# Attention in a hybrid decoder layer: the order of scores and turning in a two-deep pipeline, and the slot of the turned probabilities

## The chip, the cores and the metric

The kernel runs on one core of one Trainium2 chip. The metric is the time of one execution on the device in microseconds (us); less is better. All inputs lie in the device's memory at the start and the output lies there at the end.

## What is computed

The reference is one layer of a decoder on x of 1 x 1024 x 1024 (batch, sequence, model width), all in 32-bit floats:

```python
h = rmsnorm(x, norm1_w)
proj = h @ w_in                       # columns of mixer A, then of mixer B
# mixer A: causal short conv on q, k, v; gated delta rule over 4 heads of 128; gated RMSNorm
o_a = (rmsnorm(gated_delta_rule(qa, ka, va, g, beta), gdn_norm_w) * silu(z)).reshape(B, S, 512)
# mixer B: 8 heads of 64; causal windows (128, 1), (512, 4), (2048, 16) as (window, dilation)
o_b = dilated_attention(qb, kb, vb)   # the three branches merged by their softmax denominators
x = x + concatenate([o_a, o_b], -1) @ w_out
h = rmsnorm(x, norm2_w)
u = causal_dwconv(h @ w_up, ffn_conv_w)          # width 3, 2 x 2816 columns
x = x + (silu(u[..., :2816]) * u[..., 2816:]) @ w_down
return rmsnorm(x, final_norm_w)
```

The change concerns mixer B, the dilated attention, alone. A query at position t sees the keys t, t-d, ..., t-window of each branch; numerators and denominators of the three branches are added with a common maximum.

## The kernel before

**Layout and products.** Activations are kept transposed (channels on the 128 partitions, time along the row). Each large matrix product is made of three: both factors are split into a high part of a shorter format (fp32r) and a low rest, and hi x hi, hi x lo and lo x hi are added up in PSUM. The helper `mm3` (L196) issues such a triple, `mm` (L187) one product, `tp` (L192) one transpose by the identity matrix. In the profile all products therefore stand at L189 and all transposes at L193; most vector and scalar operations of the streams stand at L139 or L141, those of two wrappers. Which step a row belongs to is read from its tiles: `qT`, `kT` are scores, `ident` with `sm` is turning, `pt` with `vn` values, `pb` with `vc` the merge of classes, `xhi`/`xlo` with `whi`/`wlo` the dense input projection, `ohi` the output projection.

**What sets the order on TensorE (PE).** The steps of the layer are written as generators and given to a recorder, the class `Weave` (L46), with a level each. While the program is written down, the recorder keeps a model time of PE and of the other engines, of when each tile is ready and of when a buffer comes free (`product`, `account`, `slot`). A generator yields how long it will be, in the model, until its next piece can run (`need`, L95: the latest of the named tiles, less PE's model time, plus a slack); `run` (L102) takes, of the generators that are ready, the one of lowest level. So a piece that would have to wait lets pieces of other generators go ahead of it. Attention has level 5 (L1497), the output projection 8, the dense input projection 9: dense products fill the places in which attention is not ready. PE executes in exactly the recorded order (an order token on each product and transpose). The order on the other engines is chosen by a tile scheduler; the attention's softmax operations are issued through `uv` (VectorE, DVE) and `ua` (ScalarE, ACT) with high priority. The model decides the order alone; on the chip every wait is a real one.

**The attention.** There are 4 pairs of heads (`pi`), 2 halves of the sequence (`hh`), and in each half 4 blocks of 128 queries, taken two at a time (u = 0 and 2): 16 pairs of query blocks in all. One pair goes through these steps:

- `scores` (L904): for each of the two blocks and each of the two heads one product into a PSUM bank, for the near keys (the block itself and the one ahead of it), and small products for the far keys, taken in four classes by position modulo 4. The first block's two banks have the tag "asc", the second's "atr". Rows of scores are 128 and 256 columns wide in the first pair of a half-0 group, then 288/320, and 352/384 and 416/448 in half 1.
- `softmax` (L929), issued from within `scores` for each block: on DVE a reduction that adds the mask and finds the largest score, from PSUM to the tile `sm` in SBUF (a custom operation with an accumulator read behind it), one for each head; on ACT the exponentials; on DVE the reciprocal and two scalings.
- `turn` (L945): transposes `sm` on PE, head by head, into PSUM banks of the same two tags, "asc" for the first block and "atr" for the second; each of these four sets waits in the recorder with `need(pp, sm, slack=TSLACK[b])`, TSLACK (L39) being -1.0 and -0.6 us. DVE copies the near part to the tile `pt`, ACT the far part to `pb`.
- `values` (L966): 6 (first pair of a sequence) or 8 products of `pt` with the value tile `vn`, into the bank `po` of the group.
- after the second pair of a half, `merge_classes` (L975; 8 products in half 0, 16 in half 1) adds the far keys by way of `pb` and `vc`, and `give` (L989) copies the result out.

Scores, values and merge are products of plain 32-bit floats, and the trace counts two instructions for each: 20 products of scores are a row of x40, 8 of values x16, 16 of the merge x32. Transposes and dense products are counted once. A few records are missing (x10 where 12 belong).

Each PSUM tag has two banks: "hf", "asc", "ch", "atr".

**The pipeline.** `advance` (L1004) holds one pair back. Called with a new pair, it takes the pair ahead of it from the list `pipe` and does, before the change: turning of the pair ahead, scores (with softmax) of the new pair, values of the pair ahead, and at the end of a half its merge. The last call has no new pair.

**Buffers in SBUF.** `SLOTS` (L26) gives a number of slots to each tag. A tag with a star alternates between two tags, so "dv*" (L27) means two slots of "dv" and two of "dw" in turn. Before the change `sm` (one for each block) and `pt` (one for each pair) both take "dv*". The tag "uy" has five slots and holds, in the attention, q and k of a head pair (two slots for each); the four-head state tile `ct` of mixer A's chain (L798) has one of them before the attention. The lists HTAGS (L28), R1TAGS and R2TAGS (L30, L31) name the slots that the input's normalised copies and the weights of the MLP take over when the earlier users are gone; a tag named there is the slot that a tile gets, and a load into it waits for the slot's last reader.

Of the kernel before, what the change touches and what calls it, by code (L numbers as in the profile page):

```python
# [15 lines left out]
P = 128  # L16
# [6 lines left out]
APART = 0.5  # L23
KSLACK = 1.0
EPS = 1e-6
SLOTS = {"kT": 2, "kU": 2, "dv": 2, "dw": 2, "kt": 4, "uy": 5, "qa": 4, "ev": 2, "go": 2, "Xa": 7, "Xb": 9}  # L26
TURNS = {"kT*": ("kT", "kU"), "dv*": ("dv", "dw"), "X": ("Xa",) * 7 + ("Xb",) * 9}  # L27
HTAGS = ("kU", "kU", "dw", "dw", "kt", "kt", "kt", "kt", "uy", "uy", "uy", "uy", "uy", "qa", "qa", "qa", "qa",  # L28
         "ev", "ev", "go", "go") + ("Xa",) * 7
R1TAGS = ("kU", "kt", "qa", "uy", "kt", "qa", "uy", "ev", "kU", "dw", "uy")  # L30
R2TAGS = ("kt", "kt", "uy", "uy", "qa", "qa", "ev", "go", "go", "dw", "Xa")  # L31
PTAGS = ("Xb",) * 9 + ("Xa",) * 2
TOKEN = "pe"
SLACK = 3.0
# [110 lines left out]
def hybrid_layer(tc, I, out):  # L145
# [17 lines left out]
    def tile_(pool, shape, dt, name, tag, bufs):  # L163
        return wv.slot(pool.tile(list(shape), dt, name=name, tag=tag, bufs=bufs), tag, bufs)
# [3 lines left out]
    def A(name, tag, dt=F32, shape=(P, 1024)):  # L168
        if tag in TURNS:
            i = turns[tag] = turns.get(tag, -1) + 1  # L170
            tag = TURNS[tag][i % len(TURNS[tag])]
        return tile_(lp, shape, dt, name, tag, SLOTS[tag])

# [54 lines left out]
    def rsqrt(dst, src, n):  # L228
        po_.tensor_tensor(dst, src, mhalf[:, :n], op=OP.pow)
# [14 lines left out]
    def bank(tag, name="ps"):  # L244
        return tile_(pp_, (P, 512), F32, name, tag, 2)
# [10 lines left out]
    def v8(t):  # L256
        return t.rearrange("p (c t) -> p c t", c=NCH)
# [206 lines left out]
    def small(name, bufs=2):  # L464
        return tile_(sp, (P, NCH), F32, name, name, bufs)
# [316 lines left out]
    def chain_load(h, s):  # L782
        t = A("qat", "go" if s == 1 and h < 2 else "qa", shape=(P, 2, 512))
        sy.dma_start(t[:, 0, :], qpark[h][:, half(s)])
        sy.dma_start(t[:, 1, :], atpark[h][:, half(s)])
        return t

    ct = []

    def chain(h):  # L790

        for i in range(H):
            yield from wv.until(("m", i))
            yield from wv.until(("v", i))
        d = G[h]
        kT, ktok, vtok, yt, ge, rq, gq, ke = [d[n] for n in ("kT", "ktok", "vtok", "yt", "ge", "rq", "gq", "ke")]
        if not ct:
            ct.append(A("ct", "uy", shape=(P, 8, P)))  # L798
        sts = ct[0][:, 2 * h:2 * h + 2, :]
        qa = chain_load(h, 0)  # L800
        ps = bank(("asc", "ch")[h // 2])
        ms = small("ms", 4)
        tg = str(h)
        st = None
        for c in range(NCH):
            cs = slice(c * P, (c + 1) * P)
            if c == 2 and h < 2:
                qb = chain_load(h, 1)
            if c == 3 and h >= 2:
                yield from wv.until(("c", h - 2, 3))  # L810
                qb = chain_load(h, 1)
            if c == 4:
                qa = qb
            qT, at = [qa[:, i, (c % 4) * P:(c % 4 + 1) * P] for i in range(2)]
            if c == 0:
                r = vtok[:, cs]
                yield wv.need(ps, vtok, yt)
            else:
                yield wv.need(ps, st, slack=HOP)
                mm(ps[:, 0:P], kT[:, cs], st, 0.215)  # L820
                r = tile_(sp, [P, P], F32, "r", "r" + tg, 1)
                uv.scalar_tensor_tensor(r, ps[:, 0:P], ngam[:, c, h:h + 1], vtok[:, cs], op0=OP.mult, op1=OP.add)
                yield wv.need(r, slack=HOP)
            mm(ps[:, P:2 * P], yt[:, c, :], r, 0.215)
            w = tile_(sp, [P, P], F32, "w", "w" + tg, 1)
            if c < NCH - 1:
                wke = tile_(sp, [P, P], F32, "wke", "r" + tg, 1)
                uv.tensor_scalar(wke, ps[:, P:2 * P], ke[:, c:c + 1], None, op0=OP.mult)
            ua.activation(w, ps[:, P:2 * P], AF.Copy)
            if c < NCH - 1:  # L830
                yield wv.need(wke, slack=HOP)
                mm(ps[:, 2 * P:3 * P], ktok[:, cs], wke, 0.215)
                sn = sts[:, c % 2, :]
                if c == 0:
                    uv.tensor_copy(sn, ps[:, 2 * P:3 * P])
                else:
                    uv.scalar_tensor_tensor(sn, st, ge[:, c:c + 1], ps[:, 2 * P:3 * P], op0=OP.mult, op1=OP.add)
            yield wv.need(w, qa, slack=HOP)
            po = yield from next_bank("atr")
            if c:  # L840
                mm(po[:, P:2 * P], qT, st, 0.215)
            mm(po[:, :P], at, w, 0.215)

            ua.activation(vtok[:, cs], po[:, :P], AF.Copy, scale=rq[:, c:c + 1])
            if c:
                uv.scalar_tensor_tensor(vtok[:, cs], po[:, P:2 * P], gq[:, c:c + 1], vtok[:, cs], op0=OP.mult,
                                        op1=OP.add)
            if c < NCH - 1:
                st = sn
            osq = tile_(sp, [P, P], F32, "osq", "osq", 1)  # L850
            ua.activation(osq, vtok[:, cs], AF.Square, accum_out=ms[:, c:c + 1])
            wv.done.add(("c", h, c))

        ve.tensor_scalar(ms, ms, 1.0 / 128, EPS, op0=OP.mult, op1=OP.add)
        rsqrt(ms, ms, NCH)
        po_.tensor_tensor(v8(vtok), v8(vtok), ms[:, :, None].to_broadcast([P, NCH, P]), op=OP.mult)
        wv.add(1, finish(h, vtok))
# [34 lines left out]
    def attention():  # L892
# [50 lines left out]
                uv.tensor_scalar(sm[:, e, :wd], sm[:, e, :wd], den[:, e:e + 1], None, op0=OP.mult)  # L943

        def turn(pair):  # L945
            pts = A("pt", "dv*", shape=(P, 4, 256))
            for b, (it, tag) in enumerate(zip(pair, ("asc", "atr"))):
                sm, near, far = it["sm"], it["near"], it["far"]
                nf = -(-far // P)
                it["pt"] = []  # L950
                for e in range(2):
                    pt = pts[:, 2 * b + e, :]
                    it["pt"].append(pt)
                    pp = bank(tag)
                    yield wv.need(pp, sm, slack=TSLACK[b])
                    for i in range(near // P):
                        tp(pp[:, i * P:(i + 1) * P], sm[:, e, far + i * P:far + (i + 1) * P])
                    for i in range(nf):
                        tp(pp[:, near + i * P:near + (i + 1) * P], sm[:, e, i * P:(i + 1) * P])
                    uv.tensor_copy(pt[:, :near], pp[:, :near])  # L960
                    for i in range(nf):
                        rows = min(far - i * P, P)
                        ua.activation(it["pb"][e][:rows, it["u"], i, :], pp[:rows, near + i * P:near + (i + 1) * P],
                                      AF.Copy)

        def values(pair):  # L966
            yield wv.need(pair[0]["po"], *pair[0]["pt"], slack=-PSLACK)
            for it in pair:
                u = it["u"]
                for i in range(it["near"] // P):  # L970
                    for e, er in enumerate(HALVES):
                        mm(it["po"][er, u * P:(u + 1) * P], v8(it["vn"])[:, it["k0"] // P + i, er],
                           it["pt"][e][:, i * P:(i + 1) * P], 0.11, u == 0 and i == 0, False, skip_group_check=True)
# [29 lines left out]

        def advance(pair):  # L1004
            done = pipe.pop() if pipe else None
            if done is not None:
                yield from turn(done)
            if pair is not None:
                yield from scores(pair)
                pipe.append(pair)  # L1010
            if done is not None:
                yield from values(done)
                if done[1]["u"] == 3:
                    yield from merge_classes(done[0]["g"])
                    give(done[0]["g"])
# [109 lines left out]
    def hblock(name, i):  # L1125
        b = B[name][i] = block(name, HTAGS[hcount[0]])
        hcount[0] += 1
# [229 lines left out]
    def prep(stage, j):  # L1357
        if stage == 0:
# [3 lines left out]
            ops[stage, j] = list(zip(split_pair(g), split_pair(r)))  # L1362
            q = R2[j] = A("r2", R2TAGS[j], shape=(P, 2, 512))
            sy.dma_start(q[:, 0, :], upark[j][:, half(1)])
# [23 lines left out]
        else:  # L1388

            a = raw_tile("wa", ("wst", "whi")[j % 2], wd_rows(j, 1)[:, 1:2], 1)  # L1390
            ops[stage, j] = [(split_one(a[:, 0, :]), split_one(R1[j][:, 1, :], R2TAGS[j]))]

# [169 lines left out]
```

## Time and profile before

| | before |
|---|---|
| median of 3 timed runs | 1223.81 us (1223.63 to 1225.67) |
| profiled execution | 1230.37 us |
| its span | 1228.5 us |
| granted TensorE clock, mean | 0.993 |
| bytes moved by DMA | 154.80 MB, 126 GB/s mean |

The span goes from the first to the last event in the profile; the profiled execution's own time is a little longer. PE is the matrix engine, DVE the vector engine, ACT the scalar engine, POOL GpSimd; SP issues most of the DMAs. In a row of a timeline stand the start in us, the length in us, the engine, the line, the operation, out<-in by the names of the tiles, and in square brackets the idle time of the engine just before it with what ended it. x6 means that six like operations lie behind one another. PE's operations overlap (the next begins before the one ahead has ended), so in a dense stretch the distance from start to start is what a row costs. In a row of groups (line, engine, operation, tiles) come the busy time, the mean of one in ns and the idle time ahead. A row of the windows view has the stretch's start and end, its length, then busy time and (number of operations) of PE, of PE's weight loads, of DVE, ACT and POOL, the granted TensorE clock as a share of full speed, the DMA share and GB/s.

### The profile page before, as it was taken

What the parts mean: (1) busy time and instruction counts of PE and PEld (TensorE: products, weight loads), DVE (VectorE), ACT (ScalarE), POOL (GpSimd) and SP (SyncE); (2) the same over time, 40 slices, a digit from 0 to 9 for tenths busy, and PEclk for the clock granted to TensorE, in tenths of its full rate; (3) what the DMA queues carried; (4) which work ended last, traced back from release to release, by engine and by line L of the source; (5) the groups of instructions that cost most, each with busy time, mean ns of one, the idle gap of its engine ahead of it and who ended that gap; (6) DMA issues with size and microseconds to landing.
All of it is one profiled execution on the core that took longest, in us unless ns stands there. A gap on an engine that the chain in (4) does not pass through costs nothing.

```text
span 1228.5 us, 17935 instructions
## 1 busy us (share of the span) xinstructions
PE 1204.7 (98%) x6848; PEld 993.7 (81%) x6848; DVE 948.3 (77%) x1522; ACT 571.0 (46%) x1115; POOL 51.5 (4%) x58
## 2 busy tenths in 40 slices
PE   9999999999999999999999999999999999999996
PEld 7878887888877777788788888888888878787885
DVE  7675964566476778567888988889888889898875
ACT  7393344356344345555545445444444553344541
POOL 0211010003100000000000000000000000000000
PEclk9999999999999999999999999999999999999998
DMA  7325252345723303344123132231221496455523
GB/s 232 104 76 166 86 142 82 121 132 154 231 84 104 121 27 118 140 138 154 52 86 103 52 103 84 71 103 54 101 93 62 134 370 238 166 164 175 193 86 138
DMA packets 85799, 154.80 MB, mean 126 GB/s; under 512 B 21168, under 2 KB 36304, under 8 KB 85712
## 3 DMA queue, kind: packets, MB, share of 16 engines
q1 hardware_dynamic: 85712, 153.64, 38.8%
q8 instruction: 54, 0.88, 0.3%
q14 instruction: 33, 0.27, 0.1%
HBM read 117.68 MB, written 35.93 MB: 125 GB/s over the span
## 4 chain that ended last, share of the span: by engine, by line
PE 81%; DVE 8%; DMA 5%; issue 2%; ACT 2%; SPq 0%; POOLq 0%; POOL 0%; DVEq 0%; ACTq 0%
PE ps L189 42%; PE pa L189 19%; PE pc L189 9%; PE dw L189 8%; DMA wd<-in_wd 3%; PE ps L193 3%; DVE pr L139 2%; DMA r<-upark 2%; DVE wd L139 1%; DVE x1h L139 1%; DVE kT L139 1%; PE warm L189 1%; ACT dec L139 1%; DMA wst<-in_wu 0%; DVE sm L141 0%
## 5 line engine op out<-in xcount | busy, mean ns | idle before, releaser
L189 PE MATMUL dw<-pr 128*128 128x512 f32 (+1 forms) x984 | 213.4, 378 | 3.5 <-DVE x1h L139 2.3
L189 PEld LDWEIGHTS dw<-pr 128*128 128x128 f32 x984 | 176.1, 188 | 39.7 <-DVE x1h L139 4.4
L189 PE MATMUL ps<-xhi,whi 128*128 128x512 f32 x384 | 160.2, 417 | 0.0
L189 PE MATMUL ps<-xhi,wlo 128*128 128x512 f32 x384 | 150.4, 392 | 0.0
L189 PE MATMUL ps<-xlo,whi 128*128 128x512 f32 x384 | 150.2, 391 | 0.0
L189 PE MATMUL pa<-T,pair 128*128 128x512 f32 x528 | 128.7, 393 | 1.3 <-ACT u L139 1.3
L189 PEld LDWEIGHTS pa<-T,pair 128*128 128x128 f32 x528 | 100.2, 190 | 22.5 <-ACT u L139 1.6
L189 PEld LDWEIGHTS ps<-xhi,wlo 128*128 128x128 f32 x384 | 72.2, 188 | 15.7
L189 PEld LDWEIGHTS ps<-xhi,whi 128*128 128x128 f32 x384 | 72.5, 189 | 14.9 <-issue 2.6
L189 PEld LDWEIGHTS ps<-xlo,whi 128*128 128x128 f32 x384 | 72.7, 189 | 11.2
L139 ACT ACTIVATE u<-pa 128x512 f32<-128x512 f32 x44 | 26.3, 598 | 110.4 <-PE pa L189 110.4
L139 DVE SCALAR_TENSOR_TENSOR y<-xu,fcw,y 128x1023 f32<-128x1023 f32 (+1 forms) x44 | 56.4, 1281 | 25.7 <-ACT y L139 25.6
L139 ACT ACTIVATE whi<-wst 128x1024 fp32r<-128x1024 f32 (+2 forms) x42 | 43.0, 1023 | 68.8 <-PE ps L189 62.4
L189 PE MATMUL pc<-T,S 128*128 128x512 f32 x264 | 63.4, 389 | 0.0
L189 PE MATMUL pa<-B,A 128*128 128x512 f32 x264 | 63.4, 389 | 0.0
L189 PE MATMUL pc<-B,pair 128*128 128x512 f32 x264 | 63.4, 389 | 0.0
L189 PE MATMUL pa<-T,S 128*128 128x512 f32 x264 | 63.4, 389 | 0.0
L141 ACT ACTIVATE sm<-sm,mx 128x128 f32<-128x128 f32 (+7 forms) x64 | 35.5, 555 | 58.8 <-DVE mx L141 58.8
L139 DVE TENSOR_TENSOR wst<-wst 128x512 f32<-128x512 f32 x88 | 60.5, 688 | 0.8
L189 PE MATMUL ps<-B,pair 128*128 128x512 f32 x252 | 60.5, 389 | 0.0
L139 DVE TENSOR_TENSOR wlo<-wst,whi 128x1024 fp32r<-128x1024 f32 (+2 forms) x42 | 49.4, 1177 | 13.2 <-ACT whi L139 13.0
L139 ACT ACTIVATE pr<-wd 128x1024 fp32r<-128x1024 f32 x33 | 34.9, 1059 | 51.9 <-PE dw L189 23.1
(238 smaller groups left out, 2363.7 us busy)
## 6 DMA issues: line engine op xcount, KB each, us to landing
wst<-in_wu SPq DMA_DIRECT2D x44, 512.0 KB, 3.7
wd<-in_wd SPq DMA_DIRECT2D x44, 512.0 KB, 4.2
upark<-y SPq DMA_DIRECT2D x22, 512.0 KB, 3.7
wst<-in_wi SPq DMA_DIRECT2D x21, 512.0 KB, 3.7
r<-upark SPq DMA_DIRECT2D x11, 512.0 KB, 8.1
r<-upark SPq DMA_DIRECT2D x22, 256.0 KB, 7.1
wa<-in_wd SPq DMA_DIRECT2D x22, 256.0 KB, 2.7
wst<-in_wv SPq DMA_DIRECT2D x8, 512.0 KB, 3.7
```

Of the source, the lines that this page charges most:

```text
L139: return getattr(eng, op)(*a, **kw)
L141: return getattr(eng, op)(*a, **kw)
L189: tc.stamp_issue_order_token(nc.tensor.matmul(dst, lhs, rhs, start=start, stop=stop, **kw).ins, TOKEN)
L193: tc.stamp_issue_order_token(nc.tensor.transpose(dst, src, ident).ins, TOKEN)
```

## The change

In `advance` the scores of the new pair now come first, and the turning of the pair ahead follows them; values and merge stay behind turning. The tile `pt` leaves the rotating tag "dv*" and has a tag "ux" of one slot. That slot is taken from "uy", which goes from five to four; the three other users of the fifth slot (`ct`, one of HTAGS, one of R2TAGS) are named "ux".

```diff
-SLOTS = {"kT": 2, "kU": 2, "dv": 2, "dw": 2, "kt": 4, "uy": 5, "qa": 4, "ev": 2, "go": 2, "Xa": 7, "Xb": 9}
+SLOTS = {"kT": 2, "kU": 2, "dv": 2, "dw": 2, "kt": 4, "uy": 4, "ux": 1, "qa": 4, "ev": 2, "go": 2, "Xa": 7, "Xb": 9}
-HTAGS = ("kU", "kU", "dw", "dw", "kt", "kt", "kt", "kt", "uy", "uy", "uy", "uy", "uy", "qa", "qa", "qa", "qa",
+HTAGS = ("kU", "kU", "dw", "dw", "kt", "kt", "kt", "kt", "uy", "uy", "uy", "uy", "ux", "qa", "qa", "qa", "qa",
-R2TAGS = ("kt", "kt", "uy", "uy", "qa", "qa", "ev", "go", "go", "dw", "Xa")
+R2TAGS = ("kt", "kt", "uy", "ux", "qa", "qa", "ev", "go", "go", "dw", "Xa")
@@ chain
-            ct.append(A("ct", "uy", shape=(P, 8, P)))
+            ct.append(A("ct", "ux", shape=(P, 8, P)))
@@ turn
-            pts = A("pt", "dv*", shape=(P, 4, 256))
+            pts = A("pt", "ux", shape=(P, 4, 256))
@@ advance
             done = pipe.pop() if pipe else None
-            if done is not None:
-                yield from turn(done)
             if pair is not None:
                 yield from scores(pair)
                 pipe.append(pair)
             if done is not None:
+                yield from turn(done)
                 yield from values(done)
```

The orders as recorded on PE, from the first scores to the first product of the output projection, with S scores, T transposes, V values, M class merge, F dense products, and the number of each:

```
before: S4 F12 T2 F6 T4 F6 S20 V6 T12 F9 S20 V8 M8 F12 T6 F3 T6 F6 S20 V8 F15 T8 F3 T8 F6 S4 V8 M16
        ... F9 T16 V8 M16
after:  S4 F12 S20 F3 T2 F3 T4 F9 V6 S20 T12 F12 V8 M8 S20 T6 F3 T6 F12 V8 S4 T16 F9 V8 M16
        ... S20 F6 T6 F3 T6 F12 V8 M8 S20 T6 F3 T6 F12 V8 T16 F6 V8 M16 F99
```

Ahead of the attention the order is the same on every engine. F has 342 products there in both, in 44 stretches before and 28 after.

## The prediction

> **What bounds the kernel now.** I began with the page: TensorE is the busy engine, and the question is which of its microseconds are stalls that this change could take away.
>
> ```profile
> PE 1204.7 (98%) x6848; PEld 993.7 (81%) x6848; DVE 948.3 (77%) x1522; ACT 571.0 (46%) x1115; POOL 51.5 (4%) x58
> ```
>
> The PE timeline puts the attention from 329.81 us (first scores) to 484.69 us (first product of the output projection). In it, dense input-projection products fill the places between the attention's small ones. I write S, T, V, M and F for scores, turning (transposes), values, class merge and dense filler. The view of PE's waits between 325 and 510 us starts with this row:
>
> ```profile
> PE ps L193 <- DVE sm L141: 2.0, 2, 1.7
> ```
>
> So turning waits for softmax hardly ever: twice, 2.0 us. That is all the reordering can take away directly, plus what those waits drag behind them. The PE timeline at that place:
>
> ```profile
> 341.07 1.33 PE L193 MATMUL ps<-ident,sm 128*128 128x128 f32 x6 [1.74 <-DVE sm L141]
> 342.67 1.51 PE L193 MATMUL ps<-ident,sm 128*128 128x128 f32 x6 [0.26 <-DVE sm L141]
> 343.83 0.78 PE L189 MATMUL ps<-xhi,whi 128*128 128x512 f32 x1
> 344.41 0.53 PE L189 MATMUL ps<-xlo,whi 128*128 128x512 f32 x1
> 344.78 0.39 PE L189 MATMUL ps<-xhi,wlo 128*128 128x512 f32 x1
> ```
>
> The same work undisturbed, ten microseconds later (start to start: six transposes 0.57, the first F after them 0.31, the next 0.23):
>
> ```profile
> 352.58 0.82 PE L193 MATMUL ps<-ident,sm 128*128 128x128 f32 x6
> 353.15 0.47 PE L189 MATMUL ps<-xhi,whi 128*128 128x512 f32 x1
> 353.46 0.39 PE L189 MATMUL ps<-xlo,whi 128*128 128x512 f32 x1
> 353.69 0.39 PE L189 MATMUL ps<-xhi,wlo 128*128 128x512 f32 x1
> ```
>
> From 339.33 (341.07 less the gap of 1.74) to 344.78 is 5.45 us; undisturbed it is 2 x 0.57 + 0.31 + 0.23 = 1.68. The place loses 3.77 us, more than the gap, because the granted clock (ninth number: 0.50) fell to half:
>
> ```profile
> 342.00:344.00 2.00, 1.74 (x9) 1.37 (x9) 1.57 (x5) 0.53 (x2) 0.00 (x0) 0.50 0.00 0
> ```
>
> Two more places lose time: the last long S, and the last pair, which has no filler left.
>
> ```profile
> 472.74 2.60 PE L189 MATMUL ps<-kT,qT 64*128 64x256 f32 x40
> 475.27 1.09 PE L189 MATMUL ps<-pt,vn 128*64 128x128 f32 x16
> ...
> 478.48 1.91 PE L193 MATMUL ps<-ident,sm 128*128 128x128 f32 x16
> ...
> 484.69 0.50 PE L189 MATMUL ps<-ohi,whi 128*128 128x512 f32 x1
> ```
>
> Lengths elsewhere, from a short S (0.86), V of a pair (0.92) and M of a second half (1.59):
>
> ```profile
> 403.19 0.93 PE L189 MATMUL ps<-kT,qT 64*128 64x128 f32 x8
> 404.05 1.09 PE L189 MATMUL ps<-pt,vn 128*64 128x128 f32 x16
> 404.97 1.66 PE L189 MATMUL ps<-pb,vc 128*64 128x128 f32 x32
> 406.56 0.50 PE L189 MATMUL ps<-xhi,whi 128*128 128x512 f32 x1
> ```
>
> and from the long S with what follows it (1.41, 1.60 and 1.82 us for the three sizes):
>
> ```profile
> 374.07 1.47 PE L189 MATMUL ps<-kT,qT 64*128 64x256 f32 x40
> 375.48 0.77 PE L189 MATMUL ps<-pt,vn 128*64 128x128 f32 x10
> ...
> 383.31 1.68 PE L189 MATMUL ps<-kT,qT 64*128 64x256 f32 x40
> 384.91 1.09 PE L189 MATMUL ps<-pt,vn 128*64 128x128 f32 x16
> ...
> 392.89 1.89 PE L189 MATMUL ps<-kT,qT 64*128 64x256 f32 x40
> 394.71 1.09 PE L189 MATMUL ps<-pt,vn 128*64 128x128 f32 x16
> ```
>
> The S at 472.74 takes 2.53 instead of 1.82 (loss 0.71). The tail takes 6.21 instead of 16 x 0.095 + 0.92 + 1.59 = 4.03 (loss 2.18). **All stalls the change could take away: 3.77 + 0.71 + 2.18 = 6.66 us.** Everywhere else PE runs from one group into the next.
>
> **The change part by part.**
>
> *Removed.* T no longer follows the previous V, so it no longer waits for the softmax of the S before it; in the built order an S and several F lie between. I give the change all 6.66 us. The tail goes too: in the built order the attention ends 33 triples of F (99 products) before the output projection, instead of none.
>
> *Added: T behind S waits for its PSUM banks.* S takes both banks of "asc" and both of "atr"; T, now next, takes the same four. Each of its four sets of transposes must wait until the first softmax step (the custom DVE reduction) has read its bank. Before, the reductions ran under V and F. In the built order, of the 15 turns that follow an S, two follow with an F run between and thirteen directly. PE runs in order, so whatever F stands behind T waits with it. When the reductions start, in DVE's timeline:
>
> ```profile
> 375.52 0.46 DVE L141 CUSTOM_DVE_ANT_0 sm<-ps,mk 128x288 f32<-128x288 f32 x1 [2.21 <-PE ps L189]
> 375.90 0.45 DVE L141 CUSTOM_DVE_ANT_0 sm<-ps,mk 128x288 f32<-128x288 f32 x1
> ...
> 384.86 0.53 DVE L141 CUSTOM_DVE_ANT_0 sm<-ps,mk 128x352 f32<-128x352 f32 x1 [2.26 <-PE ps L189]
> 385.31 0.52 DVE L141 CUSTOM_DVE_ANT_0 sm<-ps,mk 128x352 f32<-128x352 f32 x1
> ...
> 394.55 0.59 DVE L141 CUSTOM_DVE_ANT_0 sm<-ps,mk 128x416 f32<-128x416 f32 x1 [2.52 <-PE ps L189]
> 395.06 0.59 DVE L141 CUSTOM_DVE_ANT_0 sm<-ps,mk 128x416 f32<-128x416 f32 x1
> ...
> 403.71 0.29 DVE L141 CUSTOM_DVE_ANT_0 sm<-ps,mk 128x128 f32<-128x128 f32 x1 [1.36 <-PE ps L189]
> ```
>
> Measured from the end of S (the start of PE's next row), the first reduction starts at +0.04, -0.05, -0.16 and -0.34 us, and they follow each other every 0.38, 0.45, 0.51 and about 0.22 us (the second of a pair's blocks is some 0.03 slower). A set can start about 0.2 us after its reduction's successor could (0.08 for the accumulator read, the rest my estimate of the hand-over). So, with a transpose at 0.095:
> - S of 288/320 then T of 1, 1, 2, 2: sets start at 0.62, 1.00, 1.41, 1.82 and end at 2.02, against 0.57: 1.45 lost, three times = 4.35. (The first such S has F around both halves: 0.16.)
> - S of 352/384 then twelve transposes: 0.60, 1.04, 1.52, 2.00, end 2.29 against 1.14: 1.15, twice = 2.30. Once a triple of F (0.76) stands between the halves and hides some: 0.76.
> - S of 416/448, always with that triple: 0.78, four times = 3.12.
> - Short S: the reductions are early and short: 0.10, twice = 0.20.
> - Twice other DVE work stands ahead of the reductions in the built order. At the first short S it is an aqkv scaling and a wlo split, 0.9 us late. At the last S of 352 it is wlo, zz and og, 3 x 1.15 us, of which two F triples hide most: 1.3.
>
> ```profile
> L139 DVE TENSOR_TENSOR wlo<-wst,whi 128x1024 fp32r<-128x1024 f32 x8 | 9.8, 1222 | 0.4 <-ACT whi L139 0.3
> ...
> L139 DVE TENSOR_TENSOR xr<-ps,rstdB 128x512 f32<-128x512 f32 x8 | 5.5, 686 | 0.9 <-PE ps L189 0.8
> L141 DVE DVE_READ_ACCUMULATOR2_ANT mx<- 128x1 f32 x64 | 5.3, 83 | 0.0
> ```
>
> Sum 0.16 + 4.35 + 2.30 + 0.76 + 3.12 + 0.20 + 0.9 + 1.3 = **13.1 us**. What queues behind the waiting T: its pt copies on DVE, then V. V comes two to four F triples (1.4 to 2.7 us) after T, and the copies end about 1 us after T, so V pays nothing more.
>
> *Moved: the end of dense.* The output projection now starts right behind the last dense product and needs that product's bank, which DVE empties in 0.69 (xr) after a hand-over of about 0.3, then a wlo split. PE has 0.68 us of work in another bank meanwhile, so I charge 0.45. The remaining splits stay ahead: each k step of the projection is 12 x 0.227 = 2.72 us of PE, and the og split chain (tanh, zz, og, ohi, olo: five passes of about 1.1) ends 6.9 us after dense, where k = 3 needs it at 8.6.
>
> *Fewer switches.* F runs fall from 44 to 28; the return to F costs 0.31 against 0.23, so 16 x 0.08 = 1.3 us gained. The new neighbours (S to T, V to S) have no row. Bounds 0, if they cost as much, and 2.6, if the way out of F costs the same again; I take 1.3.
>
> *Slots and queues.* Taking pt out of the rotating tag leaves sm four slots, two pairs, which the new order needs; ux is one slot, free after V, and V comes before the next T: nothing. ct moves to ux while nobody else is there: nothing. uy with four slots holds q and k of two head pairs, as before; nothing waits. On SP's queue the down-projection's loads change places by some 256 KB: 0.7 us either way where the DMAs are full, taken as 0.
>
> **Sum:** 13.1 + 0.45 - 6.66 - 1.3 = +5.6 us. The profiled execution took 1230.37 us (span 1228.5), so 1236.0; the median of the timed runs is 1223.81, so **1229.4**.
>
> **Rivals.**
> *The clock falls.* The half clock at 342 us followed one gap of 1.74 us and lasted to about 344.7, and cost roughly 3.77 less the gap and 0.3 of a second wait: 1.7 us. The change makes four stretches with 1.3 to 1.45 us of waiting within 2 us of small work; the tail's longest gap (0.8) kept the clock. If each halves it, 4 x 1.7 = 6.8 more: 1236.2. [...]
>
> *The bank waits are short and PE comes out faster.* Place: the thirteen direct S-T pairs. If only the first hand-over is paid, about 0.45 for each of 15 turns, the stalls are 6.8 and the sum 6.8 + 0.45 - 6.66 - 1.3 = -0.7; with 2.6 for the switches -2.0; with 0.3 a turn besides -4.3, 1219.5. Break-even is 7.5 us of stalls, 0.5 a turn. For it: short S costs nearly nothing. Against it: four banks, four reductions, each measured.
>
> *It does not matter.* Removed and added cancel (stalls of 5 to 10 us): 1223.8, give or take 2.4.
>
> **How the numbers follow.** A measurement here tells about 0.2%, 2.4 us, from no change. Forecast (+2.5 to +9) 0.60, clock 0.10, cancel 0.16, faster 0.14. So faster 0.14, same 0.16, slower 0.70. The range leaves out the deeper half of the faster case and the worst clock case: 1221.5 to 1235.
>
> **What would show it.** Right: PE's waits gain a row in which L193 waits for DVE's reductions (sm or mx), 10 us or more in total, mostly behind long S; the waits for softmax at 341 and for pt at 482 are gone; F stands in one block ahead of the output projection. Wrong: that row stays under 7 us, or granted clock under 1.00 in several stretches, or the output projection waiting for its splits.

## The result and the profile after

| | before | after |
|---|---|---|
| median of the timed runs, same chip | 1224.74 us (1223.63 to 1226.47, 4 runs) | 1231.80 us (1231.11 to 1232.41, 4 runs) |
| ratio to before | 1 | 1.0046, 95% interval 1.0026 to 1.0067 |
| span of the profiled execution | 1228.5 us; a second one 1222.7 us | 1229.2 us |

By the ratio on record the change makes the kernel slower by 0.46%, 5.6 us (3.2 to 8.2). The two medians of the table lie further apart, by 7.1 us or a ratio of 1.0058, which the interval includes. The forecast was +5.6.

One caution comes first. The span of the profile after is only 0.7 us above the first profile of before. That profile came from an execution that took 1230.37 us where the timed ones took 1224. A second profile of the same kernel (run *again* below) has a span of 1222.7 us. Against it the changed kernel is 6.5 us longer, 5.47 of them between the first scores and the first product of the output projection. Comparisons below use the second profile.

The busy row of the page, after, and the view of PE's waits between 325 and 510 us:

```profile
PE 1203.6 (98%) x6848; PEld 988.5 (80%) x6848; DVE 944.6 (77%) x1522; ACT 567.3 (46%) x1115; POOL 52.8 (4%) x58
```

```profile
PE ps L193 <- DVE mx L141: 5.8, 12, 0.6
```

PE is busy for 98% of the span, as before (1201.2 us in the second profile of before). In that profile the same view has three rows:

```profile
PE ps L193 <- DVE sm L141: 2.3, 2, 1.7
PE ps L189 <- DVE pt L141: 0.8, 1, 0.8
PE ps L189 <- DVE wlo L139: 0.8, 1, 0.8
```

The first two (turning for `sm`, values for `pt`) are gone. The third, a product of the output projection that waits 0.77 us for `wlo`, is still there: it only moves from 506 to 512 us, out of the view's window. One new row stands in the attention: turning waits for the reductions (`mx`) twelve times. The row does not give the whole loss, though. PE's timeline at one long S, with the T behind it:

```profile
370.51 1.68 PE L189 MATMUL ps<-kT,qT 64*128 64x256 f32 x40
372.65 1.95 PE L193 MATMUL ps<-ident,sm 128*128 128x128 f32 x12 [0.46 <-DVE mx L141]
374.36 0.48 PE L189 MATMUL ps<-xhi,whi 128*128 128x512 f32 x1
```

From the start of S to the first dense product are 3.85 us. Undisturbed, S takes 1.61 and twelve transposes 1.14, so 1.10 are lost, and the bracket shows 0.46. The rest lies between the four sets of transposes, inside the group of twelve, where each set waits for a bank of its own. DVE's timeline at the same place shows why:

```profile
372.07 0.53 DVE L141 CUSTOM_DVE_ANT_0 sm<-ps,mk 128x352 f32<-128x352 f32 x1 [2.36 <-PE ps L189]
372.52 0.08 DVE L141 DVE_READ_ACCUMULATOR2_ANT mx<- 128x1 f32 x1
372.52 0.52 DVE L141 CUSTOM_DVE_ANT_0 sm<-ps,mk 128x352 f32<-128x352 f32 x1
372.96 0.08 DVE L141 DVE_READ_ACCUMULATOR2_ANT mx<- 128x1 f32 x1
372.96 0.55 DVE L141 CUSTOM_DVE_ANT_0 sm<-ps,mk 128x384 f32<-128x384 f32 x1
373.44 0.08 DVE L141 DVE_READ_ACCUMULATOR2_ANT mx<- 128x1 f32 x1
373.44 0.55 DVE L141 CUSTOM_DVE_ANT_0 sm<-ps,mk 128x384 f32<-128x384 f32 x1
373.92 0.08 DVE L141 DVE_READ_ACCUMULATOR2_ANT mx<- 128x1 f32 x1
```

The first set of T starts at 372.65, once the first reduction and its accumulator read (372.60) are over; the fourth needs the bank of the fourth reduction, which begins at 373.44 and whose accumulator is read at 373.92. The next product starts at 374.36, some three transposes later. T ends when DVE allows it.

At the places where before lost time, the changed kernel's timeline reads: the first full pair, the last long S, the last pair.

```profile
341.45 1.95 PE L193 MATMUL ps<-ident,sm 128*128 128x128 f32 x12 [0.46 <-DVE mx L141]
343.15 0.47 PE L189 MATMUL ps<-xhi,whi 128*128 128x512 f32 x1
...
451.12 1.89 PE L189 MATMUL ps<-kT,qT 64*128 64x256 f32 x40
453.44 1.06 PE L193 MATMUL ps<-ident,sm 128*128 128x128 f32 x6 [0.42 <-DVE mx L141]
...
459.55 1.97 PE L193 MATMUL ps<-ident,sm 128*128 128x128 f32 x16
462.83 1.09 PE L189 MATMUL ps<-pt,vn 128*64 128x128 f32 x16
463.76 1.65 PE L189 MATMUL ps<-pb,vc 128*64 128x128 f32 x32
465.34 0.50 PE L189 MATMUL ps<-xhi,whi 128*128 128x512 f32 x1
...
487.92 0.39 PE L189 MATMUL ps<-ohi,whi 128*128 128x512 f32 x1
```

The tail runs without a gap, and 99 dense products (465.34 to 487.92) stand behind it. The attention as a whole, in the windows view (stretch, length, PE busy), second profile of before and after:

```profile
329.39:483.20 153.81, 150.43 (x1472) 117.67 (x1471) 115.38 (x329) 66.94 (x207) 3.48 (x18) 1.00 0.29 92
```

```profile
328.64:487.92 159.28, 153.07 (x1472) 116.89 (x1471) 109.64 (x326) 61.72 (x205) 3.41 (x18) 1.00 0.27 81
```

PE's idle time there goes from 3.4 to 6.2 us, and PE's modelled busy time, which contains the waits inside groups, grows as well. Distances from start to start tell more. Summed by kind from first scores to first product of the output projection, in us:

| kernel | S | T | V | M | F (stretches) | sum |
|---|---|---|---|---|---|---|
| before, second profile | 23.52 | 18.74 | 18.41 | 8.97 | 84.17 (44) | 153.81 |
| after | 28.67 | 23.44 | 15.11 | 8.80 | 83.26 (28) | 159.28 |
| after, TSLACK -9, -9 | 30.37 | 26.89 | 15.08 | 8.79 | 81.46 (19) | 162.59 |
| after, TSLACK 0, -9 | 22.75 | 18.93 | 15.13 | 8.78 | 83.85 (37) | 149.44 |
| values one pair later | 22.74 | 20.04 | 15.13 | 8.78 | 82.01 (25) | 148.70 |

Each group counts from its first start to the first start of the next, so a wait ahead of a group is in the group before it. S and T grow by 9.85 us, V falls by 3.30, F by 0.91, M by 0.17: +5.47.

### The profile page after: what moved, and what is told of

It reads as the page before. It is cut to its first block, busy times and chain, and to the rows that moved or that the text cites. A ratio compares the mean times of both kernels' runs of the same rounds, so it can differ in the third digit from the quotient of the medians.

```text
span 1229.2 us, 17889 instructions
## 1 busy us (share of the span) xinstructions
PE 1203.6 (98%) x6848; PEld 988.5 (80%) x6848; DVE 944.6 (77%) x1522; ACT 567.3 (46%) x1115; POOL 52.8 (4%) x58
## 4 chain that ended last, share of the span: by engine, by line
PE 82%; DVE 9%; DMA 4%; issue 2%; ACT 2%; SPq 0%; POOL 0%; POOLq 0%; DVEq 0%; ACTq 0%
PE ps L189 42%; PE pa L189 18%; PE pc L189 9%; PE dw L189 9%; PE ps L193 3%; DVE pr L139 2%; DMA wd<-in_wd 2%; DMA r<-upark 1%; DVE wd L139 1%; DVE x1h L139 1%; DVE kT L139 1%; DVE sm L141 1%; DVE wlo L139 1%; ACT dec L139 1%; DMA xt<-in_xT 0%
## 5 line engine op out<-in xcount | busy, mean ns | idle before, releaser
L189 PEld LDWEIGHTS pa<-B,A 128*128 128x128 f32 x264 | 49.5, 188 | 10.3
```

Source lines behind the costliest of these rows:

```text
L189: tc.stamp_issue_order_token(nc.tensor.matmul(dst, lhs, rhs, start=start, stop=stop, **kw).ins, TOKEN)
```

## The experiments

Theory: the loss is PE standing in T directly behind S, while DVE's four reductions free the four banks. Rivals: the slots cost it; the place of the dense products or the number of switches costs it; DVE's load costs it wherever the turns stand.

**again.** The kernel before, unchanged.

> The kernel before, unchanged, for a second profile. The first one took 1230.37 us where the timed runs took 1224, and the forecast took its 6.66 us of stalls in the attention (3.77 of them with a half clock near 342 us) from it. If these stalls belong to the kernel, first scores to first product of the output projection take 154.9 us again, with the half clock; if they, or part of them, were of that one execution, this profile's span is near 1222 and the attention is shorter (151.1 without the 3.77), and the change takes away less than was credited.

Measured: ratio 0.9998 (0.9984 to 1.0011), span 1222.7 us, attention 153.81 us. Each of the two readings was half right. The wait of 1.74 us at the first turn is there again, as are the long last S and the tail. The half clock is not. PE's timeline and the windows view of this profile:

```profile
340.66 0.84 PE L193 MATMUL ps<-ident,sm 128*128 128x128 f32 x6 [1.74 <-DVE sm L141]
342.08 0.85 PE L193 MATMUL ps<-ident,sm 128*128 128x128 f32 x6 [0.57 <-DVE sm L141]
342.68 0.47 PE L189 MATMUL ps<-xhi,whi 128*128 128x512 f32 x1
```

```profile
342.00:344.00 2.00, 1.92 (x12) 1.74 (x13) 1.31 (x4) 0.81 (x3) 0.00 (x0) 1.00 0.00 0
```

So 1.1 us of the 6.66 belonged to one execution. The other 4.7 us by which the first profile was longer lie outside the attention, as the starts of the phases in the two timelines show: 0.8 between 62 and 78 us, 1.8 in the MLP's up half, 1.9 from the down projection on. Their causes stay open.

**slots.** The renaming alone, old order:

```diff
             done = pipe.pop() if pipe else None
+            if done is not None:
+                yield from turn(done)
             if pair is not None:
                 yield from scores(pair)
                 pipe.append(pair)
             if done is not None:
-                yield from turn(done)
                 yield from values(done)
```

> The slots of the change alone (turned probabilities in ux, uy with four, the three other users renamed), in the old order. Theory that the order costs the time by PSUM bank waits: no change, 1224 within 2 us. Rival that the slots cost it (loads that wait for another last reader): about 1231.

Measured: 0.9990 (0.9978 to 1.0003). The slots cost nothing. The order carries the loss.

**new_tm9 and new_t0_9.** The changed kernel with other slacks for turning, which decide whether dense products come between S and T:

```diff
-TSLACK = -1.0, -0.6
+TSLACK = -9.0, -9.0     # new_tm9
+TSLACK = -0.0, -9.0     # new_t0_9
```

> The changed kernel with TSLACK -9, -9, so that no dense product comes between scores and turning or between the sets of turning (19 stretches of F for 28). Bank waits: the four turns behind S of 416/448 lose 1.25 for 0.73 us, three behind 352/384 1.1 to 1.3 for 0.7 to 0.9, the first turn 1.4 for 0.3, together +4.2; nine switches fewer -0.7; so about 1235.3. Rival that the loss lies in where the dense products stand or in the number of switches between kinds of products, and not in the waits: 1231 or a little less.

> The changed kernel with TSLACK 0, -9: two triples of F (1.4 us) come between long scores and turning, and one behind short scores; everything else is the same. Bank waits: the 12.3 us that the profile of the changed kernel shows behind S fall to about 1, nine more switches cost 0.7, so about 1221. Rival that the loss lies elsewhere (dense products at the end, switches): 1231.8 or 1232.5.

Measured: without any cover 1.0065 (1.0050 to 1.0080), 2.3 us above the change (the intervals overlap; in the profiles the attention is 3.3 longer); with two triples of F as cover (one behind a short S) 0.9954 (0.9936 to 0.9972), 11 us below it and 5.6 below the kernel before. The signs and sizes are those of the bank waits. By the table, S and T grow by 5.15 us without cover (4.2 expected); the fewer switches gave back 1.0, and 0.8 of a wait in F went. With cover S and T fall by 10.4. PE's timeline of new_t0_9 at the same S as above:

```profile
376.35 1.68 PE L189 MATMUL ps<-kT,qT 64*128 64x256 f32 x40
377.96 0.50 PE L189 MATMUL ps<-xhi,whi 128*128 128x512 f32 x1
...
379.24 0.39 PE L189 MATMUL ps<-xhi,wlo 128*128 128x512 f32 x1
379.47 1.47 PE L193 MATMUL ps<-ident,sm 128*128 128x128 f32 x12
380.70 0.48 PE L189 MATMUL ps<-xhi,whi 128*128 128x512 f32 x1
```

No bracket stands at the T, and twelve transposes take 1.23 us instead of the 1.71 above. Of the eight turns with twelve transposes one, the last (at 462.94 us), still takes 1.68. In the windows view PE is busy in the whole attention:

```profile
329.16:478.60 149.44, 149.44 (x1472) 117.27 (x1471) 110.25 (x326) 64.41 (x206) 3.40 (x18) 1.00 0.28 88
```

**new_t0.** As new_t0_9, with `TSLACK = 0.0, 0.0`: filler ahead of every set.

> The changed kernel with TSLACK 0, 0: dense triples stand ahead of every second set of turning as well, 52 stretches of F, and F runs out ahead of the last two pairs of query blocks (the output projection's first products fill in there). Bank waits with a price on filler: stalls behind S near 0 as with 0, -9, but 15 more returns to F (0.1 to 0.2 each, 2) and a tail without filler (2 to 3): 1224 to 1226, 1.000 to 1.002. Rival that more cover is always better: 1220.5 or less.

Measured: 1.0028 (1.0015 to 1.0040), somewhat over the expected 1.000 to 1.002. The waits behind the early S are gone, but the 342 products of F are used up ahead of the last two pairs, and what stands there waits longer than expected. The view of PE's waits:

```profile
PE ps L193 <- DVE mx L141: 3.2, 2, 2.8
PE ps L193 <- ACT pb L141: 1.8, 2, 1.3
```

Filler is a limited stock: what stands here between the sets, whose banks new_t0_9 shows to be free by then at all long turns but one, is missing at the end.

**old_t0.** The control: the slack 0, 0 in the kernel before.

> The kernel before with TSLACK 0, 0 and nothing else: a control for the slack without the new order. F then covers the first turn (the 2.6 us of waits for softmax there go), but it runs out ahead of the last half's four pairs, where the output projection's first products stand between waiting turns and values. Bank waits: the old order has none to take away, so no gain on balance, +1 to +5, 1.001 to 1.004. Rival that the slack alone made the gain of the changed kernel with TSLACK 0, -9: 0.995.

Measured: 1.0083 (1.0064 to 1.0103). The slack alone is no gain, it is a loss, and a larger one than expected. The expectation that F covers the first turn failed: F stands between its halves, and the wait ahead of the first half is there as before. Ahead of the last pairs the filler has run out, and turning waits there for `sm`, up to 3.4 us at a time. PE's timeline at the first turn, and its waits:

```profile
343.42 1.46 PE L193 MATMUL ps<-ident,sm 128*128 128x128 f32 x6 [1.74 <-DVE sm L141]
```

```profile
PE ps L193 <- DVE sm L141: 6.8, 4, 3.4
```

At three places the granted clock falls behind waits as well: at the first turn (0.98 on average from 328 to 440 us; the dense products behind the turn start 0.43 us apart, undisturbed 0.23), ahead of the last pairs (0.90 from 470 to 474, 0.78 from 474 to 480) and at the wait of 3.4 us (0.92 from 492 to 498, 0.94 from 498 to 520). By this run and *slots*, neither the slack 0, 0 nor the slots alone make a gain in the old order. The slack of new_t0_9, 0 and -9, was not run in the old order, so that its gain needs the new order is likely, not shown.

**dbl_new and dbl_old.** One suspected cost doubled: the first head's reduction of every block is done twice, in the changed kernel and in the one before.

```diff
                 uv.tensor_tensor_reduce(out=sm[:, e, :wd], ..., accum_out=mn[:, e:e + 1])
+                if e == 0:
+                    with tc.high_priority(offset=URGENT):
+                        nc.vector.tensor_tensor_reduce(out=sm[:, e, :wd], ..., accum_out=mn[:, e:e + 1])
```

> The changed kernel with the first head's softmax reduction of every block done twice (the same result; 32 reductions more, some 16 us of DVE). TensorE's order is unchanged. In the built DVE order the repeat stands two or three reductions behind the first, so the first bank of a block comes free only after four reductions. Bank waits: 0.8 to 1.0 us more behind each of 12 long scores and about 0.4 behind 3 short ones, +10 (8 to 13), about 1242. Rival that DVE's reductions are not on the path (DVE is busy 111 of the attention's 159 us): +3 or less, 1235.

> The kernel before with the same doubling. There the reductions run beside V and F: only the first turn, which waits for softmax already (1.74 us), and the last pair pay, about 1 us each, so +2.5, 1.002. If DVE's load and not the place of the turns were what costs, the doubling would cost as much as in the changed kernel: +10, 1.008.

Measured: 1.0182 (1.0165 to 1.0199) for the new order, 1.0035 (1.0017 to 1.0054) for the old one. The same work on DVE costs 17 us in one order (over its own 1.0046) and 4.3 in the other (2.5 expected), where the longest wait, at the first turn, grows from 1.74 to 2.90 us and the clock falls behind it (0.91 on average from 344 to 364 us). DVE's load is therefore not the cause; its place ahead of a waiting T is. The 17 are more than the 8 to 13 expected. From PE's timeline, S and T of 288/320 take 4.35 us for 3.36 in the changed kernel, of 352/384 4.76 for 3.85, of 416/448 4.82 for 3.69: +0.9 to 1.1, as expected, about 11 over all turns but the first. The rest is the clock, which this kernel loses at two places. The windows view at the first of them:

```profile
336.00:338.00 2.00, 0.45 (x2) 0.14 (x1) 2.00 (x6) 0.20 (x1) 0.00 (x0) 1.00 0.87 266
338.00:340.00 2.00, 1.13 (x4) 0.94 (x4) 1.91 (x11) 1.78 (x7) 0.00 (x0) 0.50 0.65 231
340.00:342.00 2.00, 2.00 (x8) 1.61 (x7) 1.49 (x7) 0.36 (x2) 0.00 (x0) 0.50 0.04 16
342.00:344.00 2.00, 2.00 (x6) 1.52 (x6) 0.62 (x3) 0.00 (x0) 0.00 (x0) 0.50 0.00 0
```

S, T and F of that turn take 11.3 us for 6.1 in the changed kernel: 5.2 more, of which waiting explains some 2. The second place costs another 1.6 in the F behind the turn.

**three.** The waits covered by other work of the attention instead of F: values and merge are held back one pair more.

```diff
         pipe = []
+        turned = []
 
         def advance(pair):
+            older = turned.pop() if turned else None
             done = pipe.pop() if pipe else None
             if pair is not None:
                 yield from scores(pair)
                 pipe.append(pair)
+            if older is not None:
+                yield from values(older)
+                if older[1]["u"] == 3:
+                    yield from merge_classes(older[0]["g"])
+                    give(older[0]["g"])
             if done is not None:
                 yield from turn(done)
-                yield from values(done)
-                if done[1]["u"] == 3:
-                    yield from merge_classes(done[0]["g"])
-                    give(done[0]["g"])
+                turned.append(done)
...
-        yield from advance(None)
+        for _ in range(2):
+            yield from advance(None)
```

> Scores first as in the change, TSLACK as in the change, but values and merge are held back one pair more: scores of the new pair, values (and merge) of the pair two ahead, then turning of the pair ahead. V (0.8 to 1.0 us) and M (0.6 or 1.6) then stand between S and T, at no cost in dense products. Bank waits: only S of 352/384 with V of 0.8 behind it leaves a wait, 0.35 four times, and the first turn 0.3; the 11.9 us of stalls fall to 1.7, so 1231.8 - 10.2 = 1221.6, beside the kernel before 0.9955 to 0.998. Rival that the order with scores first costs the time by itself (softmax on DVE beside the dense evacuations, dense products pushed to the end): 1231.8, 1.0046.

Measured: 0.9950 (0.9936 to 0.9964), just below the 0.9955 to 0.998 expected, which the interval reaches. S first is no loss when something other than T stands behind it. PE's timeline at a long S with V and M between:

```profile
363.13 1.47 PE L189 MATMUL ps<-kT,qT 64*128 64x256 f32 x40
364.53 1.09 PE L189 MATMUL ps<-pt,vn 128*64 128x128 f32 x16
365.45 1.65 PE L189 MATMUL ps<-pb,vc 128*64 128x128 f32 x32
367.04 0.87 PE L193 MATMUL ps<-ident,sm 128*128 128x128 f32 x6
367.67 0.47 PE L189 MATMUL ps<-xhi,whi 128*128 128x512 f32 x1
```

Six transposes take 0.63; behind the same S in the changed kernel they take 1.40 after a wait that lengthens S by 0.56.

**three_0.** The same with `TSLACK = 0.0, -9.0`.

> The kernel with values held back one pair more, with TSLACK 0, -9: a triple of F between V and T where banks were still late (three of the four S of 352/384; 0.29 each in the profile of that kernel), two triples instead of one ahead of the first turn (0.3), and no triple between the halves of turning behind S of 416/448. 25 stretches of F as there. Bank waits: 1 to 1.3 us better than that kernel's 0.995, so about 0.994; rival that the rest of its waits is not in those places: 0.995.

Measured: 0.9939 (0.9917 to 0.9961). The attention takes 148.19 us for 148.70, T 19.35 for 20.04. The interval covers *three* and *new_t0_9* as well, so which of the three is the fastest stays open; all three beat both kernels.

## Why the prediction was right

*What bounds the kernel.* That PE is the bound in the attention, and that only its stalls can be won, holds: with the stalls covered (new_t0_9) the attention is 4.4 us shorter, and PE has no gap left.

*Removed: 6.66 us credited, 5.5 found.* All three places are gone, as forecast. In the second profile of before they cost: the last S 0.72 over 1.82, T 0.88 at the first turn and 0.45 in the last, V and M 3.47 by the table's difference. The 1.1 too many are the half clock at 342 us, taken from one profiled execution as if it belonged to the kernel.

*Added: bank waits, 13.1 us forecast, 12.7 found.* Step by step, S and T against their undisturbed lengths: behind 288/320 1.47 each (1.45 forecast; the six transposes count 0.49 here, as in the second profile of before, and 0.57 in the forecast, by which it would be 1.39), the first one 0.32 (0.16); behind 352/384 1.09 (1.15) and with the triple 0.70 (0.76); at the last of them 0.98 (1.3), 0.8 of it as a wait of the F behind which T stands; behind 416/448 0.73 (0.78); the short ones 0.16 (0.10), the first of them 0.76 (0.9), with `aqkv` and `wlo` ahead on DVE as the built order said. The tail's sixteen transposes in one stretch take 0.14 more than in two halves. So reading the start of each reduction out of the old trace and adding a hand-over was enough. The hand-over itself was taken somewhat too long: a set was to start 0.2 us after the next reduction could, and in the rows above it is 0.13 (372.52 to 372.65).

*Moved: the output projection's start, 0.45 forecast.* From its first product to the first of the next phase are 88.86 us for 88.23: 0.63, and the timelines show both waits of the forecast. The fourth product starts at 488.86 instead of about 488.60, 0.05 after DVE's `xr` (488.12, 0.69 long) has emptied the bank; the ninth starts 0.40 behind the eighth, at 490.31, 0.05 after the `wlo` split (489.03, 1.23 long). From the end of dense (487.92) to the start of `xr` are 0.20 us, where the forecast took 0.3. The wait for `wlo` at 512 us stands in both kernels and is no cost of the change.

*Switches: 1.3 gained, bounds 0 and 2.6.* F without its one wait of 0.8 falls by 1.7 for 16 stretches fewer, 0.11 each (0.08 taken). From the 44 stretches of before to the 19 of new_tm9, F falls by 2.71, 0.11 each again.

*Sum.* 12.7 + 0.63 - 5.5 - 1.7 = +6.1 between two profiles whose spans differ by 6.5; the timed ratio says 5.6 and the two medians 7.1. The errors of the forecast (bank waits 0.4 too many, removed 1.1 too many, switches 0.4 too few, output projection 0.2 too few) nearly cancel. The steps and nearly all their sizes held; that the total agrees to the tenth is luck.

*The test named for it failed.* "Wrong: that row stays under 7 us": it stands at 5.8, and the step was right all the same. The view gives the idle time ahead of a group; three of the four waits of a turn lie between its sets and look like long transposes.

*The rivals.* The clock did not fall in the changed kernel (granted clock 1.00 in its attention), so that price was not paid; in dbl_new, with waits about 1 us longer, it was (0.50 behind one turn, 0.51 behind another). Short bank waits would have made the order a gain, 1219.5 to 1223. They are not short, but with cover (new_t0_9, 0.9954 of 1224 or 1218.4) the order is worth that much. That removed and added cancel, to 2.4 us either way, is ruled out by the interval of 3.2 to 8.2.

## What to carry to other kernels

Moving a step away from one wait puts it behind something else: look which buffers its new neighbour holds, here the same four PSUM banks, and in what order another engine gives them back. Keep a step that refills banks apart from the step that last filled them, by other ready work of one's own (here values), which uses up no filler, or by filler, which measured about the same here (0.9950 and 0.9954); and count the filler, because what covers a small wait early is missing at the end (new_t0, 1.0028). Take stalls from two profiled executions, and measure a group by start-to-start distances, since a row of waits leaves out the waits inside a group (it gave 0.46 of the 1.10 us at the S shown above).

## What the runs showed of the hardware

The clock's fall is not a matter of the wait's length alone. The same wait of 1.74 us halved the granted clock in one profile of before (0.50 from 342 to 344 us) and left it at 1.00 in the other. In old_t0 it fell behind the same wait too (F at 0.43 us a product for 0.23). In dbl_new the turns at 409 and 452 us have the same two waits, 0.88 and 0.87 us; in the windows view the clock stays behind the first of these turns and falls behind the second:

```profile
409.00:411.00 2.00, 0.75 (x4) 0.45 (x4) 2.00 (x10) 1.39 (x5) 0.00 (x0) 1.00 1.07 275
411.00:413.00 2.00, 1.94 (x11) 1.56 (x10) 1.96 (x10) 0.96 (x4) 0.00 (x0) 1.00 0.87 278
...
452.00:454.00 2.00, 1.09 (x7) 0.80 (x8) 2.00 (x10) 1.72 (x7) 0.00 (x0) 1.00 0.25 95
454.00:456.00 2.00, 2.00 (x7) 1.50 (x7) 1.89 (x8) 0.62 (x3) 0.00 (x0) 0.51 0.00 0
456.00:458.00 2.00, 2.00 (x11) 1.28 (x11) 1.52 (x3) 1.71 (x2) 0.00 (x0) 0.64 0.00 0
```

In dbl_new the half clock lasts some 3.5 us at the second place (0.51 and 0.64 in the two rows above) and over 6 at the first (0.50 from 338 to 344 us, 0.80 from 344 to 346). Among the falls are some behind waits of 0.88 with 0.87 us (dbl_new), of 1.74 (before, old_t0) and of 3.40 (old_t0). Why like waits end in both ways is not shown by these runs.
